# Three quarters of the first adaptive condition on TensorE, one quarter on VectorE

## The chip, the cores and the metric

The kernel runs on one core of a Trainium2 chip. The metric is device time in microseconds (us). Engines are called PE (TensorE, whose weight loads are listed apart as PEld), DVE (VectorE), ACT (ScalarE), POOL (GpSimd) and SP, which issues most DMA transfers.

## The reference

One block of a latent backbone: adaptive normalisation, two kinds of scanned attention, an output projection and a gated feed-forward. 2048 latent tokens of width 1024 and 256 context tokens go through the same weights. Only its beginning matters here:

```python
mod_x = (jax.nn.silu(c) @ w_ada[l] + b_ada[l])[:, None, :]
mod_c = jax.nn.silu(c_ctx) @ w_ada[l] + b_ada[l]
shx1, scx1, gx1, shx2, scx2, gx2 = jnp.split(mod_x, 6, -1)
shc1, scc1, gc1, shc2, scc2, gc2 = jnp.split(mod_c, 6, -1)
fc = mixer_features(modulate(rmsnorm(h_ctx, g_mix[l]), shc1, scc1), ...)
fx = mixer_features(modulate(rmsnorm(x, g_mix[l]), shx1, scx1), ...)
```

The first of the six parts, the shift, is columns 0 to 1023 of the product, the second, the scale, columns 1024 to 2047. These 2048 columns of `w_ada` (8 MB in fp32) are needed before any token can be normalised; the 4096 others come later and are not touched. There are two vectors to multiply with them, one for the latents and one for the context (c = 0 and c = 1 in the code).

## The kernel before

`w_ada`'s first 2048 columns arrive in eight slices of 128 rows (k = 0 to 7, 1 MB each) in the tiles `area0` to `area3`, two slices to a tile. Each slice has four column blocks of 512. Blocks 0 and 1 (the shift) go to PE: the two vectors, padded to 32 columns in `csl`, are the stationary operand, and the sums over k stand as rows in two PSUM tiles `mrow`. An fp32 matmul of this form shows as two records in the trace. Blocks 2 and 3 (the scale) go to DVE: for each vector and block it multiplies the slice with a scalar per partition and adds it to an accumulator `dacc` (arena tiles 12 to 15, shown as arena_93 to arena_96), four passes a slice. The sum over the partitions is still to be done then.

Meanwhile ACT squares the context (`ctxv`, shown as area_101), POOL adds the squares up, and `rstd` and `diag` make a diagonal matrix of the context's inverse norms (tile gm), which `rows_bc` multiplies with ones on PE to broadcast them over the partitions: `bc_ctx`.

After the last slice PE turns the condition into columns, in one PSUM tile `mps`: the accumulators by 16 matmuls with a column of ones, the rows `mrow` (copied to SBUF by ACT, tiles `mrs`) by 8 matmuls with the identity. DVE adds the bias, which gives `modc`, and makes `a1` and `b1` of it; with them and `bc_ctx` the context is modulated (`modulate`), split in a high and a low part for PE, and multiplied with the first weights: the gate weights and the first key unit (tile w). Between lie the sums over the partitions of the first latent block's squares (`x0s`, arena tiles 4 and 5, shown as arena_85 and arena_86): ACT squares, DVE and POOL add, PE sums.

Every engine runs its instructions in order. Program order is that in which the code issues them, but a scheduler that simulates the engines' times lists them anew before the program is built; so a change at the start may move instructions further on. The tiles of the pool gm (5 buffers), of w (4) and of the raw weights wr (3) are used in turn. The trace gives line 193 to nearly all instructions, a helper's line, so rows are told apart by their tiles.

Of the kernel before, what the change touches and what calls it, by code (L numbers as in the profile page):

```python
# [16 lines left out]
ALU = mybir.AluOpType  # L17

P = 128
D = 1024  # L20
KT = 8
T = 2048
TCX = 256
NB = 4
BT = 512
# [57 lines left out]
def pack(i):  # L83
# [69 lines left out]
    ident=(P, P), mneg=(P, 2, P), lmask=(P, len(LEVELS) * 128), tri=(P, 2 * P))  # L153
# [45 lines left out]
def block_kernel(ctx: ExitStack, tc: tile.TileContext, I, out):  # L199
    nc = tc.nc  # L200
    load = Load()
    V, G, S, PE = [Metered(e, load, k) for e, k in ((nc.vector, "V"), (nc.gpsimd, "G"), (nc.scalar, "S"), (nc.tensor, "PE"))]
# [19 lines left out]
    def ctile(shape, name, dt=F32, pool=const):  # L222
        return pool.tile(shape, dt, name=name)
# [10 lines left out]
    def M_(shape=(P, BT)):  # L234
        return gen.tile(list(shape), F32, name="gm", tag="gm", bufs=BUFS["gm"])
# [11 lines left out]
    def flat(i):  # L247
        return arena[i].rearrange("p a b -> p (a b)")[:, :BT]
# [15 lines left out]
    def MM():  # L264
        return pmm.tile([P, BT], F32, name="mm")

    def PS(shape=(P, BT)):
        return pps.tile(list(shape), F32, name="ps")

    def small(n):  # L270
        return sm.tile([P, n], F32, name=f"sm{n}", tag=f"sm{n}")
# [4 lines left out]
    def loaded(name, shape, dt=F32, pool=const):  # L276
        t = ctile(shape, name, dt, pool)
        dma(t, I[name])
        return t
# [7 lines left out]
    def cs(c):  # L287
        return slice(c * P, (c + 1) * P)

    pc = loaded("pc", [P, NPC])  # L290
    ident = loaded("ident", [P, P])
# [26 lines left out]
    ones = ctile([P, P], "ones")  # L318
# [8 lines left out]
    csl = csl_.rearrange("p (k c) -> p k c", c=32)  # L327
# [58 lines left out]
    def rstd(t, n, r):  # L386

        nj = n // P
        ps = PS()
        ts = t if isinstance(t, list) else [t]  # L390
        for j in range(nj):
            for i, t in enumerate(ts):
                PE.matmul(ps[:, 2 * j:2 * j + 2], t[:, cs(j)], ones[:, 0:2], start=(i == 0), stop=(i == len(ts) - 1))
        V.tensor_scalar(r[:, :nj], ps[:, 0:2 * nj:2], 1.0 / D, EPS, ALU.mult, ALU.add)
        G.tensor_tensor(r[:, :nj], r[:, :nj], mhalf[:, :nj], ALU.pow)

    def diag(t, n, r):
        for j in range(n // P):
            V.tensor_scalar(t[:, cs(j)], ident, r[:, j:j + 1], None, ALU.mult)

    def rows_bc(t, n):
        bc = PS()
        PE.matmul(bc[:, :n], ones, t[:, :n], start=True, stop=True)
        return bc
# [12 lines left out]
    def sq_sums(x, n, engs):  # L417

        ts = [flat(4 + k)[:, :n] for k in range(KT)]
        m = len(engs)  # L420
        for k in range(KT):
            S.activation(ts[k], x(k), AF.Square)
            if k >= m:
                engs[k % m].tensor_tensor(ts[k % m], ts[k % m], ts[k], ALU.add)
        return ts[:m]

    mrow = [MM(), MM()]
    dacc = {(q, c): flat(12 + 2 * q + c) for q in range(2) for c in range(2)}
    rc_ = small(4)
    late_x = []  # L430
    for k in range(KT):
        ak = ada[k // 2][:, k % 2]
        for q in range(2):
            m = PE.matmul(mrow[q][0:32], csl[:, k], ak[:, q * BT:(q + 1) * BT], start=(k == 0), stop=(k == KT - 1))
            for c in range(2):
                a = ak[:, D + q * BT:D + (q + 1) * BT]
                if k == 0:
                    V.tensor_scalar(dacc[q, c], a, csl[:, k, c:c + 1], None, ALU.mult)
                else:
                    V.scalar_tensor_tensor(dacc[q, c], a, csl[:, k, c:c + 1], dacc[q, c], ALU.mult, ALU.add)  # L440
        late_x.append(m)
        if k == 3:
            ct_ = sq_sums(lambda i: ctxv[:, i], TCX, [G])
        if k == 6:
            rstd(ct_, TCX, rc_)
            ct_ = M_()
            diag(ct_, TCX, rc_)
    bc_ctx = rows_bc(ct_, TCX)
    modc = ctile([P, 48, 2], "modc")
    mps = PS()  # L450
    for u in range(8):
        for c in range(2):
            o = 16 + 4 * u + 2 * c
            PE.matmul(mps[:, o:o + 2], dacc[u // 4, c][:, cs(u % 4)], ones[:, 0:2], start=True, stop=True)
    mrs = [M_() for _ in range(2)]
    for q in range(2):
        S.copy(mrs[q][0:32], mrow[q][0:32])
    for u in range(8):
        PE.matmul(mps[:, 2 * u:2 * u + 2], mrs[u // 4][0:32, cs(u % 4)], ident[0:32, 0:2], start=True, stop=True)
    bada = pc[:, C_BADA:C_BADA + 16, None].broadcast_to([P, 16, 2])  # L460
    V.tensor_tensor(modc[:, 8:16], mps[:, 16:48].rearrange("p (u c two) -> p u c two", c=2, two=2)[:, :, :, 0],
                    bada[:, 8:16], ALU.add)
    a1 = ctile([P, 2, KT], "a1")
    b1 = ctile([P, 2, KT], "b1")
    for c in (1, 0):
# [1729 lines left out]
```

## Time and profile before

| | |
|---|---|
| median of three runs | 2883.23 us (2871.2 to 2886.63) |
| profiled execution | 2878.33 us, of which 2876.5 us are the profile's span |
| busy over the span | PE 92%, DVE 65%, POOL 60%, ACT 48% |
| chain that ended last | PE 51%, DVE 18%, DMA 13%, ACT 6% |
| mean granted clock of PE | 0.96 of full speed |

The shares are means over stages with different limits. The change lies in the first 50 us, and there the time from the last slice of `w_ada` to the first matmul on the context is to be read, engine by engine; the stage after that shows what an earlier start of it is worth.

### The profile page before, as it was taken

The numbers are of one execution on the slowest core, as the hardware profiler recorded it, in microseconds if no ns is written. First come the engines' busy times: TensorE is split into PE (matmuls) and PEld (weight loads), VectorE is DVE, ScalarE is ACT, GpSimd is POOL, SyncE is SP. The second block draws the span as 40 slices with busy tenths as digits, with TensorE's granted clock in tenths as the row PEclk, the third lists the DMA queues.
The fourth block names the chain that finished last, engine by engine and source line by source line (L and its number), as shares of the span: only waits on it lengthen the run. The fifth ranks groups of instructions, "written<-read, shape, count | busy, mean of one in ns | idle before, by whom it ended". The sixth has DMA issues, their size and how long they took to land.

```text
span 2876.5 us, 44314 instructions
## 1 busy us (share of the span) xinstructions
PE 2634.8 (92%) x13592; PEld 2212.8 (77%) x13592; DVE 1877.0 (65%) x3893; ACT 1388.7 (48%) x3367; POOL 1725.9 (60%) x2323
## 2 busy tenths in 40 slices
PE   6999989898989888988999999889997999998898
PEld 4888979787878767876788888667785888886777
DVE  7578778865864345788788544777656444447775
ACT  4666654544545556665556334334443333343343
POOL 4676533345455345758666556777756655557773
PEclk7999999899999999998999999999998999999999
DMA  6764534476666777753334322423572332224212
GB/s 262 241 192 144 161 81 135 134 209 205 195 201 195 212 211 227 240 154 95 119 117 141 128 86 79 140 73 97 190 251 77 116 101 88 85 76 144 73 59 88
DMA packets 295916, 418.44 MB, mean 145 GB/s; under 512 B 38654, under 2 KB 181278, under 8 KB 292992
## 3 DMA queue, kind: packets, MB, share of 16 engines
q1 hardware_dynamic: 288320, 397.42, 44.6%
q0 software_dynamic: 7360, 18.19, 1.9%
q8 instruction: 108, 1.77, 0.3%
q14 instruction: 128, 1.05, 0.1%
HBM read 304.99 MB, written 110.49 MB: 144 GB/s over the span
## 4 chain that ended last, share of the span: by engine, by line
PE 51%; DVE 18%; DMA 13%; issue 6%; ACT 6%; POOL 4%; SPq 1%; DVEq 0%; POOLq 0%; ACTq 0%
PE mm L193 46%; DVE arena L193 6%; DVE area L193 6%; PE ps L193 5%; DVE gm L193 4%; ACT arena L193 2%; POOL w L193 2%; DVE xall L193 2%; DMA area<-in_wada_dram 2%; DMA arena<-d_nm 2%; DMA arena<-d_bt 1%; POOL arena L193 1%; SPq L207 1%; ACT area L193 1%; ACT ps L193 1%
## 5 line engine op out<-in xcount | busy, mean ns | idle before, releaser
L193 PE MATMUL mm<-area,w 128*128 128x512 f32 (+2 forms) x8264 | 1988.0, 398 | 96.5 <-DVE area L193 39.3
L193 PEld LDWEIGHTS mm<-area,w 128*128 128x128 f32 (+1 forms) x8264 | 1554.1, 193 | 440.2 <-DVE area L193 40.8
L193 POOL TENSOR_TENSOR w<-area,w 128x256 fp32r<-128x256 f32 x572 | 453.2, 815 | 294.7 <-ACT w L193 271.6
L193 POOL TENSOR_TENSOR w<-wr,w 128x256 fp32r<-128x256 f32 (+2 forms) x484 | 386.6, 818 | 163.1 <-ACT w L193 146.9
L193 POOL TENSOR_TENSOR arena<-arena 128x128 f32<-128x128 f32 (+1 forms) x520 | 232.9, 471 | 192.2 <-DMA arena<-d_bt 52.7
L193 ACT CAST w<-area 128x512 fp32r<-128x512 f32 x286 | 177.0, 620 | 287.4 <-PE mm L193 260.8
L193 PE MATMUL ps<-arena,arena 128*128 128x129 f32 (+2 forms) x1700 | 232.4, 294 | 60.3 <-ACT arena L193 20.1
L193 PEld LDWEIGHTS ps<-arena,arena 128*128 128x128 f32 (+1 forms) x1700 | 210.8, 194 | 83.3 <-ACT arena L193 26.6
L193 PE MATMUL mm<-w,area 128*128 128x256 f32 x1728 | 228.5, 289 | 2.8 <-DVE gm L193 1.4
L193 ACT CAST w<-wr 128x512 fp32r<-128x512 f32 (+3 forms) x272 | 158.0, 583 | 146.5 <-PE mm L193 74.4
L193 DVE TENSOR_TENSOR area<-area 128x512 f32<-128x512 f32 (+1 forms) x214 | 160.0, 761 | 104.1 <-DMA area<-in_wgu_dram 58.1
L193 PEld LDWEIGHTS mm<-w,area 128*128 128x128 f32 x1728 | 216.7, 194 | 5.3 <-DVE gm L193 1.6
L193 DVE TENSOR_TENSOR arena<-ps,arena 64x128 f32<-64x128 f32 (+1 forms) x512 | 154.9, 303 | 94.3 <-ACT ps L193 67.5
L193 DVE TENSOR_TENSOR gm<-mm,gm 128x512 f32<-128x512 f32 (+3 forms) x136 | 93.0, 684 | 160.2 <-PE mm L193 131.6
L193 DVE SCALAR_TENSOR_TENSOR gm<-mm,pc,gm 128x441 f32<-128x441 f32 (+4 forms) x328 | 187.7, 596 | 8.0 <-ACT edge L193 5.2
L193 DVE SCALAR_TENSOR_TENSOR area<-mm,modc,area 128x512 f32<-128x512 f32 (+1 forms) x184 | 131.4, 721 | 85.4 <-PE mm L193 85.3
L193 DVE TENSOR_TENSOR arena<-arena,arena 128x256 f32<-128x256 f32 (+3 forms) x170 | 128.6, 766 | 57.7 <-ACT arena L193 27.8
L193 ACT COPY gm<-mm 128x512 f32<-128x512 f32 (+3 forms) x183 | 104.0, 571 | 118.2 <-PE mm L193 115.6
L193 ACT ACTIVATE ps<-arena 128x256 f32<-128x256 f32 x224 | 85.2, 385 | 129.4 <-DVE xall L193 89.4
L193 PEld LDWEIGHTS ps<-arena,xall 128*128 128x128 f32 x896 | 117.9, 197 | 26.7 <-issue 5.0
L193 PE MATMUL ps<-arena,xall 128*128 128x64 f32 x896 | 122.1, 277 | 16.2 <-DVE xall L193 6.9
L193 DVE TENSOR_TENSOR xall<-ps,arena 64x128 f32<-64x128 f32 x448 | 129.2, 289 | 7.0
(179 smaller groups left out, 3046.7 us busy)
## 6 DMA issues: line engine op xcount, KB each, us to landing
area<-in_wgu_dram SPq DMA_DIRECT2D x170, 256.0 KB, 2.7
d_ff<-gm SPq DMA_DIRECT2D x88, 256.0 KB, 2.0
arena<-d_ff SPq DMA_DIRECT2D x88, 256.0 KB, 2.8
wr<-in_win_dram SPq DMA_DIRECT2D x72, 256.0 KB, 4.0
wr<-in_wout_dram SPq DMA_DIRECT2D x64, 256.0 KB, 3.7
arena<-d_kq SPq DMA_DIRECT2D x112, 128.0 KB, 3.0
area<-in_wada_dram SPq DMA_DIRECT2D x24, 512.0 KB, 5.1
arena<-d_bt SPq DMA_DIRECT2D x80, 128.0 KB, 2.8
```

Source lines behind the costliest of these rows:

```text
L193: return f(out, *args, **kw)
L207: return nc.sync.dma_start(o, i)
```

## The change

PE takes three column blocks (the shift, and the first half of the scale), DVE one. The rows of PE are turned into columns first, then the accumulators, and `bc_ctx` is issued after both instead of before. The bias is added in three pieces instead of two.

```diff
--- before.py
+++ after.py
@@ -424,20 +424,20 @@
                 engs[k % m].tensor_tensor(ts[k % m], ts[k % m], ts[k], ALU.add)
         return ts[:m]
 
-    mrow = [MM(), MM()]
-    dacc = {(q, c): flat(12 + 2 * q + c) for q in range(2) for c in range(2)}
+    mrow = [MM() for _ in range(3)]
+    dacc = [flat(12 + c) for c in range(2)]
     rc_ = small(4)
     late_x = []
     for k in range(KT):
         ak = ada[k // 2][:, k % 2]
-        for q in range(2):
+        for q in range(3):
             m = PE.matmul(mrow[q][0:32], csl[:, k], ak[:, q * BT:(q + 1) * BT], start=(k == 0), stop=(k == KT - 1))
-            for c in range(2):
-                a = ak[:, D + q * BT:D + (q + 1) * BT]
-                if k == 0:
-                    V.tensor_scalar(dacc[q, c], a, csl[:, k, c:c + 1], None, ALU.mult)
-                else:
-                    V.scalar_tensor_tensor(dacc[q, c], a, csl[:, k, c:c + 1], dacc[q, c], ALU.mult, ALU.add)
+        for c in range(2):
+            a = ak[:, 3 * BT:]
+            if k == 0:
+                V.tensor_scalar(dacc[c], a, csl[:, k, c:c + 1], None, ALU.mult)
+            else:
+                V.scalar_tensor_tensor(dacc[c], a, csl[:, k, c:c + 1], dacc[c], ALU.mult, ALU.add)
         late_x.append(m)
         if k == 3:
             ct_ = sq_sums(lambda i: ctxv[:, i], TCX, [G])
@@ -445,21 +445,22 @@
             rstd(ct_, TCX, rc_)
             ct_ = M_()
             diag(ct_, TCX, rc_)
-    bc_ctx = rows_bc(ct_, TCX)
     modc = ctile([P, 48, 2], "modc")
     mps = PS()
-    for u in range(8):
+    mrs = [M_() for _ in range(3)]
+    for q in range(3):
+        S.copy(mrs[q][0:32], mrow[q][0:32])
+    for u in range(12):
+        PE.matmul(mps[:, 2 * u:2 * u + 2], mrs[u // 4][0:32, cs(u % 4)], ident[0:32, 0:2], start=True, stop=True)
+    for u in range(12, 16):
         for c in range(2):
-            o = 16 + 4 * u + 2 * c
-            PE.matmul(mps[:, o:o + 2], dacc[u // 4, c][:, cs(u % 4)], ones[:, 0:2], start=True, stop=True)
-    mrs = [M_() for _ in range(2)]
-    for q in range(2):
-        S.copy(mrs[q][0:32], mrow[q][0:32])
-    for u in range(8):
-        PE.matmul(mps[:, 2 * u:2 * u + 2], mrs[u // 4][0:32, cs(u % 4)], ident[0:32, 0:2], start=True, stop=True)
+            o = 24 + 4 * (u - 12) + 2 * c
+            PE.matmul(mps[:, o:o + 2], dacc[c][:, cs(u % 4)], ones[:, 0:2], start=True, stop=True)
+    bc_ctx = rows_bc(ct_, TCX)
     bada = pc[:, C_BADA:C_BADA + 16, None].broadcast_to([P, 16, 2])
-    V.tensor_tensor(modc[:, 8:16], mps[:, 16:48].rearrange("p (u c two) -> p u c two", c=2, two=2)[:, :, :, 0],
-                    bada[:, 8:16], ALU.add)
+    V.tensor_tensor(modc[:, 12:16], mps[:, 24:40].rearrange("p (u c two) -> p u c two", c=2, two=2)[:, :, :, 0],
+                    bada[:, 12:16], ALU.add)
+    V.tensor_tensor(modc[:, 8:12], mps[:, 16:24].rearrange("p (u c) -> p u c", c=2), bada[:, 8:12], ALU.add)
     a1 = ctile([P, 2, KT], "a1")
     b1 = ctile([P, 2, KT], "b1")
     for c in (1, 0):
```

On PE, around the last slices (area_105 holds slices 6 and 7; arena_85 is the context's sum of squares; `ps<-ident,gm` turns rows into columns, `ps<-gm,ones` is bc_ctx, `ps<-ones,arena_93` an accumulator's sum):

```order
 L193 MATMUL ps<-ones,arena_85 128x2 x2
-L193 MATMUL mm<-area_105,arena_81 32x512 x4
+L193 MATMUL mm<-area_105,arena_81 32x512 x6
+L193 MATMUL ps<-ident,gm 128x2 x4
 L193 MATMUL ps<-gm,ones 128x256
+L193 MATMUL ps<-ident,gm 128x2 x8
 L193 MATMUL ps<-ones,arena_93 128x2
 L193 MATMUL ps<-ones,arena_94 128x2
```

Twelve transposing matmuls stand now ahead of the accumulators' sums, around the broadcast; before, eight stood behind the sums, of which there were 16 and are now 8.

On DVE, the last two slices of the accumulation (sm holds the context's inverse norms, the rows with ident make the diagonal matrix):

```order
-L193 TENSOR_SCALAR sm_168<-ps 128x2
+L193 TENSOR_SCALAR sm_169<-ps 128x2
+L193 TENSOR_SCALAR gm<-ident,sm_169 128x128 x2
 L193 SCALAR_TENSOR_TENSOR arena_93<-area_105,arena_81,arena_93 128x512
 L193 SCALAR_TENSOR_TENSOR arena_94<-area_105,arena_81,arena_94 128x512
-L193 SCALAR_TENSOR_TENSOR arena_95<-area_105,arena_81,arena_95 128x512
-L193 SCALAR_TENSOR_TENSOR arena_96<-area_105,arena_81,arena_96 128x512
-L193 TENSOR_SCALAR gm<-ident,sm_168 128x128 x2
 L193 TENSOR_TENSOR arena_85<-arena_85,arena_87 128x512
```

The diagonal matrix is made ahead of the last slice's passes instead of behind them, and two of four passes a slice are gone.

On ACT, where the context's modulation ends (area_101 and its high part), in the program before (area_416 are the tokens of latent block 1, whose squares are summed; `gm<-mm 32x256` copies the gates' first result; area_280 and area_472 are block 0 and its high part; CAST w makes the high part of a weight tile):

```order
L193 ACTIVATE area_101<-area_101,b_274 128x256 x2
L193 ACTIVATE area_416,rx_336<-area_416 128x1024 x2
L193 COPY gm<-mm 32x256
L193 ACTIVATE area_416,rx_336<-area_416 128x1024 x2
L193 CAST arena_329<-gm 98x512
L193 ACTIVATE gm<-mm,pc 16x256
L193 CAST w<-wr 128x512 x2
L193 ACTIVATE area_472<-area_280,b_274 128x512
```

and in the changed one, where area_408 are the same tokens and area_272 and area_464 the same block and its high part:

```order
L193 ACTIVATE area_101<-area_101,b_266 128x256 x2
L193 COPY gm<-mm 32x256
L193 ACTIVATE area_408,rx_328<-area_408 128x1024 x2
L193 ACTIVATE gm<-mm,pc 16x256
L193 ACTIVATE area_464<-area_272,b_266 128x512
L193 ACTIVATE area_408,rx_328<-area_408 128x1024 x2
L193 ACTIVATE area_464<-area_272,b_266 128x512
L193 CAST arena_321<-gm 98x512
L193 ACTIVATE area_464<-area_272,b_266 128x512
L193 CAST w<-wr 128x512
```

All four squaring passes and three activations of block 0 stand now between the copy and the next weight cast; before it was two passes and none.

Beyond the start both programs hold the same instructions on every engine, but for two more table loads on ACT. Their order differs in places: on PE in the first sixth of its instructions and between a fifth and a half of them, by up to some 70 places; from the middle to the end it is the same. On SP transfers move by up to 27 places.

## Rows read from the trace of the kernel before

**Rows 1.** The page: span, and busy time of each engine with its instructions.

```profile
span 2876.5 us, 44314 instructions
...
PE 2634.8 (92%) x13592; PEld 2212.8 (77%) x13592; DVE 1877.0 (65%) x3893; ACT 1388.7 (48%) x3367; POOL 1725.9 (60%) x2323
```

**Rows 2.** TensorE in the timeline: start us, us, engine, what, count, idle before it.

```profile
6.39 7.04 PE L193 MATMUL mm<-area,arena 128*32 128x512 f32 x12 [6.39 <-DMA area<-in_wada_dram]
...
21.18 1.90 PE L193 MATMUL mm<-area,arena 128*32 128x512 f32 x4 [0.54 <-DMA area<-in_wada_dram]
24.05 0.61 PE L193 MATMUL ps<-ones,arena 128*128 128x2 f32 x4 [0.96 <-POOL arena L193]
24.58 3.62 PE L193 MATMUL mm<-area,arena 128*32 128x512 f32 x8
34.38 1.22 PE L193 MATMUL ps<-gm,ones 128*128 128x256 f32 x2 [6.17 <-DVE gm L193]
...
42.15 3.57 PE L193 MATMUL ps<-ident,gm 32*128 32x2 f32 x16
45.65 3.58 PE L193 MATMUL ps<-ones,arena 128*128 128x2 f32 x16
49.09 6.11 PE L193 MATMUL mm<-area,w 128*112 128x256 f32 x28
...
59.38 6.40 PE L193 MATMUL mm<-area,w 128*128 128x256 f32 x36 [3.33 <-ACT w L193]
```

**Rows 3.** One of TensorE's first weight loads in the timeline.

```profile
8.07 0.18 PEld L193 LDWEIGHTS mm<-area,arena 128*32 128x32 f32 x1 [0.68 <-issue]
```

**Rows 4.** VectorE in the timeline, from the last slices to the condition.

```profile
29.17 3.74 DVE L193 SCALAR_TENSOR_TENSOR arena<-area,arena,arena 128x512 f32<-128x512 f32 x4
32.84 1.49 DVE L193 TENSOR_SCALAR gm<-ident,sm 128x128 f32<-128x128 f32 x2
...
45.76 0.26 DVE L193 TENSOR_TENSOR modc<-ps,pc 128x16 f32<-128x16 f32 x2 [9.24 <-PE ps L193]
```

**Rows 5.** ScalarE in the timeline, 26 to 60 us.

```profile
28.24 0.57 ACT L193 COPY gm<-mm 32x512 f32<-32x512 f32 x1 [0.28 <-PE mm L193]
28.72 4.52 ACT L193 ACTIVATE arena<-area 128x512 f32<-128x512 f32 x8
...
51.59 1.04 ACT L193 ACTIVATE area<-area 128x1024 f32<-128x1024 f32 x1
52.53 0.19 ACT L193 ACTIVATION_READ_ACCUMULATOR area<-area 128x1 f32 x1
...
55.23 0.36 ACT L193 COPY gm<-mm 32x256 f32<-32x256 f32 x1 [1.47 <-PE mm L193]
...
58.21 0.47 ACT L193 ACTIVATE gm<-mm,pc 16x256 f32<-16x256 f32 x1
58.70 1.14 ACT L193 CAST w<-wr 128x512 fp32r<-128x512 f32 x2
59.75 0.72 ACT L193 ACTIVATE area<-area,b 128x512 fp32r<-128x512 f32 x1
```

**Rows 6.** GpSimd in the timeline: the last sum of block 0's squares.

```profile
36.23 1.41 POOL L193 TENSOR_TENSOR arena<-arena,arena 128x512 f32<-128x512 f32 x1
```

**Rows 7.** Stretches: length, busy us of PE, PEld, DVE, ACT, POOL; clock; DMA.

```profile
28.30:34.30 6.00, 0.00 (x0) 0.00 (x0) 6.00 (x10) 5.85 (x12) 4.14 (x3) 0.67 1.06 401
34.30:49.00 14.70, 14.62 (x66) 14.41 (x66) 5.25 (x17) 2.60 (x7) 4.91 (x9) 0.50 0.77 303
56.00:80.00 24.00, 17.55 (x91) 15.09 (x90) 23.71 (x35) 19.60 (x36) 19.77 (x22) 0.79 0.21 69
80.00:100.00 20.00, 19.85 (x97) 16.40 (x98) 11.36 (x14) 9.90 (x20) 12.39 (x14) 1.00 0.76 244
450.00:1600.00 1150.00, 1037.62 (x5663) 884.47 (x5663) 797.34 (x2075) 641.06 (x1871) 639.29 (x1006) 0.96 0.58 175
```

**Rows 8.** Waits between 450 and 1600 us: total us, times, longest.

```profile
POOL arena L193 <- DMA arena<-d_nm: 60.1, 30, 5.5
```

## The prediction

> **What bounds the kernel now.** I read the page first: PE is busy 92% of a span of 2876.5 us [rows 1]. A mean like that says nothing of the first 50 us, so next came PE's own timeline there. The reader should see two gaps in it. Up to 28.2 us PE runs the row matmuls as the slices land: the last eight records start at 24.58 and take 3.62 us. Then nothing for 6.17 us, released by DVE, until the context's broadcast at 34.38 [rows 2]. DVE explains it: its passes over the last slice run from 29.17 for 3.74 us, although PE had finished with that slice at 28.2, and the diagonal matrix follows at 32.84 with 1.49 us [rows 4]. So at this place DVE is the engine that ends last. From 34.38 on PE is the bound, with small matmuls: broadcast, 32 records of sums, 16 of transposes, and DVE waits 9.24 us for them before it can add the bias at 45.76 [rows 2, 4]. Behind them PE sums block 0's squares (45.65, 3.58 us) and starts on the context at 49.09 [rows 2].
>
> The stretches say what the stage after that hangs on: from 56 to 80 us DVE is busy 23.71 of 24 us, PE 17.55 and ACT 19.60; from 80 to 100 PE is busy 19.85 of 20 [rows 7]. And PE waits 3.33 us for a weight tile from ACT before 59.38 [rows 2].
>
> **The change, part by part.** Sixteen of DVE's 32 accumulating passes go. At 3.74/4 = 0.94 us [rows 4] these are some 15 us of DVE work, but most of it ran while slices were still landing; on the path it frees only the gap of 6.17 us.
>
> PE gets 8 more row matmuls, 16 records. With six records a slice instead of four it falls behind the loads. The first four records go at the low rate, 0.18 + 0.68 = 0.86 us apart [rows 3], two more at 1.90/4 = 0.475 [rows 2]: slice 0 ends at 6.39 + 3.44 + 0.95 = 10.8. Five slices of 6 x 0.475 = 2.85 us bring slice 5's end to 25.0; its load was there by 21.18 [rows 2], so no load is waited for. The context's sums take 0.61 (POOL had delivered at 24.05), and slices 6 and 7 twelve records of 3.62/8 = 0.45, 5.4 us. PE ends the rows at 31.1 instead of 28.2: 2.9 us later. This is not hidden; it is paid out of the gap.
>
> DVE is then in time: the sum of squares is on PE at 25.6 instead of before slice 6, the diagonal matrix takes 1.49, the last two passes 1.9 [rows 4]. Even with a microsecond or two for GpSimd's power function between, it is done by 31, when PE has 24 transposing records ahead of the accumulators.
>
> The third copy on ACT starts at 31.1 and takes 0.57 [rows 5]; eight records from the first row tile cover it. Block 0's squares (28.72, 4.52 us [rows 5]) stand behind the copies on ACT and start at 31.7, 2.9 us later; POOL's last sum of them, which ended at 36.23 + 1.41 = 37.6 [rows 6], moves with them to 40.5.
>
> Small records: 24 transposes and 16 sums replace 16 and 32. At the price of the row of transposes, 3.57/16 = 0.22 us [rows 2], that is 5.4 + 3.6 us, with 1.2 for the broadcast 10.1 us, from 31.1 to 41.2. The condition is there at 41.3 instead of 45.76, 4.5 us earlier. POOL's sum (40.5) is just in time, and block 0's 16 records of 3.58 us end at 44.8: the context starts 4.4 us earlier than 49.09.
>
> What is that worth? The copy of the gates' result on ACT moves from 55.23 to 50.8. But the order behind it has changed. Before, the next weight cast began 58.70 - 55.23 = 3.5 us after the copy began. Now copy (0.36), four squaring passes with their reads (4 x 1.04 + 4 x 0.19, less some overlap, 4.9), the gates' activation (0.47), three of block 0's activations (0.72 each) and a cast (0.6, half of 1.14) stand ahead of it [rows 5]: 8.5 us. The cast begins at 59.3, 0.6 later than before, and PE, waiting for it before 59.38 [rows 2], resumes 0.6 later, not 4.4 earlier. Against that, ACT has three activations (2.2 us) behind it that before came after the cast, and DVE, the engine that is busy all the time from 56 to 80, can start on block 0 4.4 us earlier. If DVE's work sets the end of this stage, 4.4 us are kept; if the weight casts do, 0.6 us are lost. The two row readings bound it, and nothing in the rows sits nearer to one than the other, save that ACT's 2.2 us of finished work must come back. I take 2 us kept.
>
> The rest of the program holds the same instructions in another order. The trace of before can't show the new order. I take nothing for it, and as its bounds a tenth of PE's idle time in the reordered stretch: 1150 - 1037.6 = 112 us are idle between 450 and 1600 [rows 7], so 11 us either way. Two more table loads on ACT, which is busy 48% of the span [rows 1], cost nothing where it idles.
>
> **The sum.** Gap -6.2, late rows +2.9, small records -1.2 (10.1 instead of 11.4 from 34.38 to 45.76), start of the context -4.4, kept 2. The profiled execution took 2878.3 us, 1.8 us more than its span, and would take 2876. The median of the runs is 2883.2, 4.9 us above the profiled one, so I predict 2881. The runs shown spread over 15 us, 0.5%, which is about what a measurement can tell from no change.
>
> **A rule weighed.** In the rows PE's clock falls in the gap (mean 0.67 of 2.4 GHz from 28.3 to 34.3) and then stays at 0.50, the level of 1.2 GHz, from 34.3 to 49 us, although PE is busy 14.62 of these 14.7 us with small matmuls [rows 7]. The same kind of record took 0.61/4 = 0.15 us at 24.05, at full clock, against 0.22 [rows 2]. The Trainium skill's "TensorE: Matmul & The Clock Gate", section "Why this matters for your kernels", advises to keep TensorE busy without idle gaps to get and keep the full clock. By that advice the removed gap would keep the clock up; the rows show that busy time of this kind does not bring it up, and whether it holds it up no row shows.
>
> **The rivals.**
>
> *Hidden in part (forecast).* 2881, own range 2872 to 2889. Chance 0.42.
>
> *The whole head gain is kept.* DVE decides from 56 to 80, which its 23.71 of 24 us speak for [rows 7]; against it speaks the late weight cast. 2883.2 - 4.4 = 2879. Chance 0.15.
>
> *The clock stays up.* With no gap, the small records run at 0.15 us: 24 and 16 of them and the broadcast take 6.7 us, to 37.8; now POOL's sum at 40.5 decides, and 16 records of 0.15 end at 43.0, 6.1 us earlier than before. Weight cast 1.1 earlier, middle of the two 3.6: 2880. For it speaks that the gap is gone, against it the 14.7 us at half clock in spite of work [rows 7]. Chance 0.15. The skill's advice above is this rival.
>
> *ACT's order makes it slower.* Place: the four squaring passes ahead of the weight cast at 59 us. If the context starts no earlier than before, because PE's rows or the late squares take more than I think, the cast comes 8.5 - 3.5 = 5 us later, and so does the next unit: 2888. It decides once the gain at the head is under 2 us. Chance 0.10.
>
> *A reordered scan is slower or faster.* SP's transfers move by up to 27 places. Between 450 and 1600 us POOL waits 30 times for loads of d_nm, 60.1 us in all, 2.0 us a time [rows 8]. If the new order delays these by half a microsecond each, that is 15 us: 2898; as much the other way gives 2868. Chance 0.06 and 0.12 (the simulated order was made for an earlier start, which the early part then has). That the change does not do what it says is excluded by the new order: rows and passes are there.
>
> **How the numbers follow.** The likeliest is 2881. The cases of under 5 us all lie between 2872 and 2890 with the spread of the runs; the reordering's bounds of 11 us around 2881 widen this to 2866 and 2893, outside which lie most of the last rival's two ends and little else, under 2 in 10. Faster by over 0.5% (under 2868.8) is the fast end of the reordering and a little of the clock: 0.14. Slower by over 0.5% (over 2897.6) is its slow end: 0.06. Within: 0.80.
>
> **What would show it.** In the new profile the row matmuls should end near 31 and the small records follow without a gap; DVE's bias near 41; the first context matmul near 45; ACT's weight cast near 59, with PE waiting about 8 us for it. Small records of 0.15 instead of 0.22 would be the clock's rival. If PE's long stretch before 100 us begins 4 us earlier, the whole gain was kept. A time outside the range would mean that the order between 450 and 1600 us matters more than the change itself, and would stand in PE's idle time there.

## The result: 0.8% slower

The changed kernel took 2900.23 us in the median of six runs (2893.68 to 2903.5), the kernel before, timed with it, 2876.84 us (2871.16 to 2886.63). The ratio is 1.0079, interval [1.0066, 1.0092]. The prediction, 2881 us between 2866 and 2893 with a chance of 0.06 for slower, was wrong.

What makes it odd stands in the first 60 us. They became better than predicted. TensorE in the timeline of the changed kernel (start us, us, engine, what, count, idle before it):

```profile
24.69 0.61 PE L193 MATMUL ps<-ones,arena 128*128 128x2 f32 x4
25.23 5.34 PE L193 MATMUL mm<-area,arena 128*32 128x512 f32 x12
30.50 1.05 PE L193 MATMUL ps<-ident,gm 32*128 32x2 f32 x8
31.48 0.70 PE L193 MATMUL ps<-gm,ones 128*128 128x256 f32 x2
32.10 1.94 PE L193 MATMUL ps<-ident,gm 32*128 32x2 f32 x16
33.98 2.23 PE L193 MATMUL ps<-ones,arena 128*128 128x2 f32 x16
36.91 0.59 PE L193 MATMUL ps<-ones,arena 128*128 128x2 f32 x2 [0.70 <-DVE arena L193]
38.07 3.15 PE L193 MATMUL ps<-ones,arena 128*128 128x2 f32 x14 [0.57 <-POOL arena L193]
41.08 0.75 PE L193 MATMUL mm<-area,w 128*112 128x256 f32 x2
...
55.20 3.76 PE L193 MATMUL mm<-area,w 128*128 128x256 f32 x14 [7.25 <-ACT w L193]
```

The 6.17 us gap of [rows 2] is gone; the row matmuls end at 30.57 and the small ones follow. The context begins at 41.08 where it began at 49.09, 8.0 us earlier. But the stretch at 55.20, which stood at 59.38 [rows 2], waits 7.25 us for ScalarE's weight tile instead of 3.33, so 4.2 us are left of the 8.0. VectorE and ScalarE at these places, in the same view:

```profile
26.50 0.48 DVE L193 TENSOR_SCALAR gm<-ident,sm 128x128 f32<-128x128 f32 x2 [0.84 <-POOL sm L193]
...
36.78 0.31 DVE L193 TENSOR_TENSOR modc<-ps,pc 128x8 f32<-128x8 f32 x3
```

```profile
47.12 0.36 ACT L193 COPY gm<-mm 32x256 f32<-32x256 f32 x1 [3.26 <-PE mm L193]
...
54.55 0.60 ACT L193 CAST w<-wr 128x512 fp32r<-128x512 f32 x1
```

The condition is there at 36.78 (45.76 before [rows 4]), the copy at 47.12 (55.23 [rows 5]), but the cast only at 54.55 (58.70 [rows 5]).

Where, then, are the 23 us lost? I laid the two traces beside each other, TensorE's records counted from the end (beyond the start the programs hold the same matmuls, though not in the same order). The changed kernel is some 8 us ahead at 43 to 53 us, 4 ahead at 59, level at 85 to 108, 7 behind at 330, 9 behind at 350 to 400, 8 to 16 behind up to 1110, 19 at 1212, 22 to 25 from 1300 to the end. There is no single place. The stretches of the changed kernel (length, busy us of PE, PEld, DVE, ACT, POOL; clock; DMA):

```profile
60.00:300.00 240.00, 214.71 (x1520) 196.72 (x1519) 162.01 (x399) 149.97 (x359) 159.36 (x237) 0.94 0.56 180
450.00:1600.00 1150.00, 1030.45 (x5634) 874.86 (x5633) 789.25 (x2066) 631.66 (x1844) 627.60 (x998) 0.96 0.57 172
```

and the first of them in the kernel before:

```profile
60.00:300.00 240.00, 221.85 (x1581) 202.55 (x1581) 172.44 (x429) 156.62 (x378) 169.35 (x253) 0.95 0.58 185
```

From 60 to 300 us TensorE is busy 7.1 us less than before, and gets through 61 records fewer; from 450 to 1600 us 7.2 us less (1037.62 [rows 7]). Over the whole span its busy time is even longer, 2645.7 against 2634.8 us [rows 1]. Of these 10.9 us the changed head with its 8 more records makes 1.4; from the first context matmul on the same 13491 records took longer, 2612.6 instead of 2603.2 us:

```profile
span 2899.9 us, 44344 instructions
...
PE 2645.7 (91%) x13600; PEld 2212.8 (76%) x13600; DVE 1869.7 (64%) x3878; ACT 1394.3 (48%) x3370; POOL 1723.8 (59%) x2323
```

So idle time grew by 12.5 us and busy time by 10.9. The longer busy time is not a chance of two traces: from the first context matmul on TensorE is busy 2601.0 to 2606.5 us in three traces with the old order throughout (before, `bias_three_pieces`, `new_head_old_order`) and 2612.6 to 2618.4 us in four with the new one (the changed kernel, `split31_old_sequence`, `split22_new_sequence`, `old_head_new_order`); the runs follow below.

### The profile page after: what moved, and what is told of

It is laid out like the page before. It is cut to its first block, busy times and chain, and to the rows that moved or that the text cites. A ratio compares the mean times of both kernels' runs of the same rounds, so it can differ in the third digit from the quotient of the medians.

```text
span 2899.9 us, 44344 instructions
## 1 busy us (share of the span) xinstructions
PE 2645.7 (91%) x13600; PEld 2212.8 (76%) x13600; DVE 1869.7 (64%) x3878; ACT 1394.3 (48%) x3370; POOL 1723.8 (59%) x2323
## 4 chain that ended last, share of the span: by engine, by line
PE 37%; DVE 7%; POOL 2%; DMA 2%; issue 2%; ACT 1%; DVEq 0%; POOLq 0%; ACTq 0%; SPq 0%
PE mm L193 36%; DVE area L193 4%; DVE arena L193 1%; PE ps L193 1%; POOL w L193 1%; DVE gm L193 1%; DMA area<-in_wgu_dram 0%; POOL arena L193 0%; POOL area L193 0%; DMA gm<-d_o 0%; ACT w L193 0%; DVE xall L193 0%; DMA gm<-d_x 0%; ACT area L193 0%; ACT arena L193 0%
## 5 line engine op out<-in xcount | busy, mean ns | idle before, releaser
L193 PE MATMUL mm<-area,w 128*128 128x512 f32 (+1 forms) x8264 | 1992.0, 398 | 99.7 <-DVE area L193 38.5
L193 DVE TENSOR_TENSOR area<-area 128x512 f32<-128x512 f32 (+1 forms) x214 | 164.4, 781 | 111.2 <-DMA area<-in_wgu_dram 57.2
```

The costliest lines, as they stand in the source:

```text
L193: return f(out, *args, **kw)
```

## The experiments

**Theory A:** the head gains, and the order in which the scheduler lists the instructions behind it loses more. **Theory B:** the loss comes from the head itself, from what it computes and when, and from the moved broadcast above all. The twelve kernels besides the changed one were timed in five rounds beside the kernel before, in three series (its medians there 2870.8, 2870.22 and 2872.41 us); the changed kernel's row is the result above. Kernels of different series are compared by their ratios. "Old" and "new" are the orders of the program before and of the changed one; the stretches part at about 300 and 720 us.

| run | head | order to 300 us / to 720 us / behind | median us | ratio to before |
|---|---|---|---|---|
| new_head_old_order | changed | old / old / old (forced) | 2866.61 | 0.9984 [0.9972, 0.9995] |
| new_head_new_old_old | changed | new / old / old (forced) | 2878.74 | 1.0024 [1.0015, 1.0033] |
| new_head_new_new_old | changed | new / new / old (forced) | 2878.92 | 1.0027 [1.0014, 1.0040] |
| new_head_old_old_new | changed | old / old / new (forced) | 2881.55 | 1.0031 [1.0021, 1.0041] |
| new_head_old_new_new | changed | old / new / new (forced) | 2882.25 | 1.0042 [1.0026, 1.0058] |
| changed kernel | changed | new / new / new | 2900.23 | 1.0079 [1.0066, 1.0092] |
| old_head_new_order | before's | new / new / new (forced) | 2898.95 | 1.0100 [1.0082, 1.0118] |
| split31_old_sequence | split only | new / new / new | 2895.97 | 1.0079 [1.0065, 1.0093] |
| split22_new_sequence | sequence only | new / new / new | 2893.21 | 1.0066 [1.0053, 1.0079] |
| bias_three_pieces | before's | old, some places apart | 2871.52 | 1.0001 [0.9989, 1.0013] |
| adders_swapped | changed, one edit | nearly new / old / old | 2880.29 | 1.0031 [1.0017, 1.0045] |
| b1_on_gpsimd | changed, one edit | a third / old / old | 2874.46 | 1.0005 [0.9995, 1.0015] |
| new_order_two_places_undone | changed | new, two places old (forced) | 2891.39 | 1.0069 [1.0049, 1.0089] |

### Head and order exchanged

To force an order, the kernel holds a table of the other program's sequence on each of the five engines, from block 0's load on, and ties each instruction behind its predecessor on its engine. The ties set the order only; no engine waits for another because of them. No run forces a program's own order, so a cost of the ties alone is not measured. Against one that matters speak two pairs below: `adders_swapped`, which forces nothing, has 1.0031 where the forced kernel of nearly the same order has 1.0027, and the forced `new_order_two_places_undone` is no slower than the changed kernel.

```diff
+def pin_order(nc, tc, base):
...
+    left = np.frombuffer(zlib.decompress(base64.b85decode(PIN)), "<i2").astype(np.int64).tolist()
...
+        for a, b in zip(v, v[1:]):
+            tc.add_manual_dep(made[f"I-{base + b}"], f"I-{base + a}", nosync, reason="order of another program")
...
     while any(queue[k] or active[k] for k in KINDS):
         after_step()
+    pin_order(nc, tc, pin_base)
```

The changed head with the old order:

> The changed kernel, with all instructions from block 0's load on forced, engine by engine, into the order that the kernel before has (issue order alone, no added waits). Theory A (the loss of 23 us is the scheduler's new order, the change itself gains at the head): not slower than before, 2865 to 2877 us, the first context matmul at about 41 us. Theory B (the change itself costs the time, through what its earlier start collides with): about 2900 us as the changed kernel.

Measured 0.9984 [0.9972, 0.9995], 2866.61 us. TensorE from 40 us on in this run:

```profile
40.83 0.75 PE L193 MATMUL mm<-area,w 128*112 128x256 f32 x2
41.87 4.74 PE L193 MATMUL mm<-area,w 128*112 128x256 f32 x26 [0.29 <-DVE area L193]
46.44 1.02 PE L193 MATMUL ps<-gm,ones 128*128 128x512 f32 x2
50.79 6.40 PE L193 MATMUL mm<-area,w 128*128 128x256 f32 x36 [3.33 <-ACT w L193]
```

The wait for the weight tile is 3.33 us again, as in [rows 2], and the stretch starts 8.6 us earlier than at 59.38 there. What is left of that at the end is 0.16%, 4 to 5 us in the medians.

The head before with the new order:

> The kernel before, with its old start, and from block 0's load on forced into the order that the changed kernel has. Theory A: about 2900 us or some us more, since the order's loss is there without the head's gain of 8 us. Theory B: 2877 us, as before.

Measured 1.0100 [1.0082, 1.0118], 2898.95 us. The new order loses 1.0% behind the old head, and 0.95% behind the new one (0.9984 to 1.0079). That is theory A, and against B: the order costs 27 to 29 us (of 2870). The change to the head gains 0.16% with the old order, with an interval from 0.05 to 0.28%; the 0.21% between the two heads with the new order is about as large as its own uncertainty.

A part of the order's loss goes with TensorE's clock. Over all runs the mean granted clock was 0.9584 to 0.9593 in the five kernels with the new order throughout (one of them with two places put back), and 0.9611 to 0.9627 in the kernel before and the eight others. With the two levels 1.00 (2.4 GHz) and 0.50 (1.2 GHz) this is 235 to 241 us at the lower level against 214 to 223. My estimate from these numbers is that some 19 us more at half clock, in which half as much gets done, cost up to 9 us of the loss. What in the order lowers the clock no run shows.

### Which stretch of the order

The same table, with the other program's sequence up to or from a place in each engine's list (TensorE's 2000th and 3715th instruction behind block 0's load, near 300 and 720 us). First the old order up to 300 us, then the old order from 720 us on:

> The changed kernel, with the order of the kernel before up to about 300 us and its own order from there on (between 300 and 530 us both orders agree). Theory A: what was lost up to 350 us (from 8 us ahead to 8 us behind in the traces, 16 us) comes back, the loss after 1100 us (12 us) stays: 2884 to 2890 us. Theory B: 2900 us.

> The changed kernel in its own order up to about 720 us and in the order of the kernel before from there to 1400 us, where they come to agree again. Theory A: the loss of 12 us after 1100 us comes back, the early one stays: 2886 to 2890 us. Theory B: 2900 us.

Measured 1.0042 (2882.25 us) and 1.0027 (2878.92 us). Both medians lie below the ranges in us, which I had reckoned from 2877 us for the kernel before; it took 2870.8 in this series. As ratios to 2877 the ranges are 1.0024 to 1.0045 and 1.0031 to 1.0045, so the first holds and the second was missed by 0.04%: the late order costs a little more than I expected. By these runs the early order is worth 0.37%, the late one 0.52%. Whether these add up, and the mirror images:

> The changed kernel with the order behind the start forced: as in the program before up to about 720 us, as in the changed one from there on (there TensorE's projections, mm, stand some 25 matmuls later and the scan's, ps, some 49 earlier than before, for most of the stretch from 770 to 1210 us). Theory A (losses of the stretches add): the whole old order gave 0.9984, the old order from 720 us on gave back 0.0052, so this gives 0.9984 + 0.0052 = 1.0036 (1.002 to 1.005), with the lag behind the old order's trace growing between 750 and 1350 us. Theory C (the middle only loses what the early part set late): 0.998 to 1.000.

> The mirror image: the changed kernel with the changed order up to about 300 us and the old one behind it. Theory A: the old order gave 0.9984, the early part's order costs 0.0037, so 1.002 (1.0005 to 1.0035); the lag behind the old order's trace stands at 10 to 16 us from 320 us to the end. If the early lag is a slack that is made up later (theory D): 0.998 to 1.000.

Measured 1.0031 [1.0021, 1.0041] and 1.0024 [1.0015, 1.0033], against 1.0036 and 1.002 expected. Alone, the late order costs 1.0031 - 0.9984 = 0.47% and the early one 0.40%; the order between 300 and 720 us costs 0.03% (1.0027 to 1.0024) or 0.11% (1.0042 to 1.0031). So the losses add, within the intervals of some 0.1% a run, and neither is slack of the other: theories C (the late part loses only what the early part set late) and D (the early lag is made up later) fall.

What the late stretch's order does to the waits, from 740 to 1340 us (total us, times, longest), first with the old order throughout:

```profile
POOL arena L193 <- DMA arena<-d_nm: 54.5, 27, 5.1
...
ACT ps L193 <- DMA arena<-d_nm: 26.3, 11, 9.8
DVE arena L193 <- ACT ps L193: 23.9, 27, 4.2
```

then with the new order behind 720 us (new_head_old_old_new):

```profile
POOL arena L193 <- DMA arena<-d_nm: 75.3, 31, 7.9
...
DVE arena L193 <- ACT ps L193: 46.9, 27, 6.6
...
ACT ps L193 <- DMA arena<-d_nm: 39.5, 11, 9.1
PEld ps L193 <- issue: 32.2, 16, 4.6
```

By the order itself, for most of 770 to 1210 us TensorE's projection matmuls (mm) stand 25 places later in the new list and the scan's (ps) 49 places earlier on average, and ScalarE's weight casts 30 later. The scan then has fewer projections ahead of it, and its engines wait more for one another. Over all fourteen traces the clearest sign of the late stretch's order is VectorE's wait for ScalarE in the scan (DVE arena <- ACT ps, 740 to 1340 us): 19.6 to 24.9 us in the seven traces with the old order there, 43.7 to 50.8 in the seven with the new one. TensorE's weight loads for the scan (PEld ps <- issue) part likewise, 15.5 to 20.2 against 25.2 to 32.2. GpSimd's wait for the loads of d_nm does not: 46.5 to 67.3 against 57.2 to 79.2. That the scan's place is the mechanism within the stretch fits the rows, but no run moves the two streams alone.

### Two places of the early stretch

The trace of the changed kernel shows two waits there that are longer than before's: for the weight cast (7.25 us against 3.33, above), and at the late condition's sum, for a product that GpSimd makes (5.54 us against 0.50):

```profile
154.23 0.56 PE L193 MATMUL ps<-ones,area 128*128 128x2 f32 x2 [5.54 <-POOL area L193]
```

The new order was forced, with these two places as before (ScalarE and TensorE):

```diff
+ACTIVATE area_408,rx_328<-area_408 128x1024 x2
 COPY gm<-mm 32x256
-ACTIVATE area_408,rx_328<-area_408 128x1024 x2
+CAST w<-wr 128x512
 ACTIVATE gm<-mm,pc 16x256
...
-CAST w<-wr 128x512
```

```diff
+MATMUL mm<-area_289,w 128x256
 MATMUL ps<-ones,area 128x2
...
-MATMUL mm<-area_289,w 128x256 x24
+MATMUL mm<-area_289,w 128x256 x23
```

> The changed kernel in its own order, fixed, save two places at which its trace showed TensorE waiting: on ScalarE the weight cast stands directly behind the copy of the gates' result again, with two of the four squaring passes ahead of the copy (place 1), and on TensorE the late condition's sum and the three sums behind it stand behind the first matmul of the next unit again (place 2). Theory A1 (these two places make the early part's loss of some 11 us): the cast begins near 48.5 instead of 54.55 us, TensorE waits some 2 us instead of 7.25 for it and 0.5 instead of 5.5 for the sum near 154, and 8 to 11 us come back: ratio to before 1.004 to 1.005. Theory A2 (the loss is spread over the order, what comes back at one place is lost at the next): under 4 us come back, ratio 1.0065 to 1.009.

Measured 1.0069 [1.0049, 1.0089]. ScalarE and TensorE in this run:

```profile
48.22 0.61 ACT L193 CAST w<-wr 128x512 fp32r<-128x512 f32 x1
```

```profile
55.31 1.65 PE L193 MATMUL mm<-area,w 128*128 128x256 f32 x6 [4.64 <-ACT w L193]
58.29 4.00 PE L193 MATMUL mm<-area,w 128*128 128x256 f32 x17 [1.32 <-POOL w L193]
...
151.05 0.28 PE L193 MATMUL ps<-ones,area 128*128 128x2 f32 x2
...
170.34 0.56 PE L193 MATMUL ps<-ones,area 128*128 128x2 f32 x2 [4.54 <-POOL arena L193]
```

The cast came at 48.22, 6.3 us earlier, but TensorE had work for eight matmuls and then waited 4.64 us for the next cast; the sum at 151.05 waited no longer, but the one at 170.34 waited 4.54 us. What came back at one place was lost at the next. The median speaks for A2 (under 4 us), but the interval holds 1.0079 too, so that anything came back is not shown; A1's 8 to 11 us (1.004 to 1.005) lie at and beyond its other edge. The early loss hangs on no one wait that I found, and its cause within the order stays open.

### Parts of the change, with the scheduler left free

The split alone, with the sequence of the code as before:

```diff
+    bc_ctx = rows_bc(ct_, TCX)
     modc = ctile([P, 48, 2], "modc")
     mps = PS()
+    for u in range(12, 16):
...
     mrs = [M_() for _ in range(3)]
...
-    for u in range(12, 16):
...
-    bc_ctx = rows_bc(ct_, TCX)
```

> The change's split alone (three column blocks on TensorE, one on VectorE, bias in three pieces), with the code's sequence as before: the context's broadcast first, then the accumulators' sums, then the rows turned into columns. The scheduler lists this program beyond the start in the same order as the changed kernel. Theory A (the order behind the start decides): slower than before like the changed kernel, ratio 1.006 to 1.010, whatever the head gains. Theory B (the head's own sequence decides, the late broadcast above all): without the moved broadcast the loss goes away, ratio 0.997 to 1.000. In the trace A expects the first context matmul near 41 to 43 us as in the changed kernel, and TensorE's wait of some 7 us for the weight cast before about 56 us again.

Measured 1.0079 [1.0065, 1.0093], the number of the changed kernel, with the context at 40.95 us and the wait for the weight tile of 7.25 us again:

```profile
27.92 0.70 PE L193 MATMUL ps<-gm,ones 128*128 128x256 f32 x2
28.55 2.76 PE L193 MATMUL mm<-area,arena 128*32 128x512 f32 x6
...
40.95 0.75 PE L193 MATMUL mm<-area,w 128*112 128x256 f32 x2
...
55.20 3.75 PE L193 MATMUL mm<-area,w 128*128 128x256 f32 x14 [7.25 <-ACT w L193]
```

Theory B's late broadcast is out: it stands here, at 27.92, ahead of the last slice's matmuls, and nothing changes.

The sequence alone, with two blocks for each engine as before:

```diff
-    bc_ctx = rows_bc(ct_, TCX)
     modc = ctile([P, 48, 2], "modc")
     mps = PS()
-    for u in range(8):
...
     mrs = [M_() for _ in range(2)]
...
+    for u in range(8):
...
+    bc_ctx = rows_bc(ct_, TCX)
```

> The change's sequence alone: two blocks on TensorE and two on VectorE as before, but rows turned into columns first, then the accumulators' sums, the broadcast last. The head hardly moves, since VectorE still ends late: the first context matmul between 47 and 50 us. The scheduler's order behind it is a third one, neither that of before nor that of the changed kernel. Theory A: the time is that of a third draw, anywhere within 1% of before, and not to be told from the head; a ratio outside 0.998 to 1.002 with a head that stays would be for it. Theory B (the head's start decides): ratio 0.999 to 1.001.

Measured 1.0066 [1.0053, 1.0079], and this expectation was wrong twice. Behind the start its list is not a third one: on four engines it is the changed kernel's, place for place, and on ScalarE but for one swapped pair. And the head moved:

```profile
28.40 1.94 PE L193 MATMUL ps<-ident,gm 32*128 32x2 f32 x16
30.27 0.38 PE L193 MATMUL ps<-ones,arena 128*128 128x2 f32 x2
30.89 6.56 PE L193 MATMUL ps<-ones,arena 128*128 128x2 f32 x30 [0.23 <-DVE arena L193]
37.32 1.20 PE L193 MATMUL ps<-gm,ones 128*128 128x256 f32 x2
38.31 3.41 PE L193 MATMUL ps<-ones,arena 128*128 128x2 f32 x16
41.58 6.50 PE L193 MATMUL mm<-area,w 128*112 128x256 f32 x28
```

The context starts at 41.58, almost as early as with the whole change. VectorE is as late as before, but TensorE no longer stands waiting for it with the broadcast; it fills the time with the rows and then the accumulators. So either half of the change removes the gap, and either half brings the scheduler to the same new order.

An edit worth nothing at the head, as a control:

```diff
-    V.tensor_tensor(modc[:, 8:16], mps[:, 16:48].rearrange("p (u c two) -> p u c two", c=2, two=2)[:, :, :, 0],
-                    bada[:, 8:16], ALU.add)
+    scale = mps[:, 16:48].rearrange("p (u c two) -> p u c two", c=2, two=2)[:, :, :, 0]
+    V.tensor_tensor(modc[:, 12:16], scale[:, 4:8], bada[:, 12:16], ALU.add)
+    V.tensor_tensor(modc[:, 8:12], scale[:, 0:4], bada[:, 8:12], ALU.add)
```

> The kernel before with one edit that gives and takes next to nothing: the bias of the scale's 8 columns is added in two VectorE instructions of 4 columns in place of one of 8 (one instruction of about 0.13 us more). The scheduler's order behind it is again another one. Theory A: the time is that of another draw, and may differ from before by up to 1% either way although the head is the same to 0.3 us; theory B (a time comes from what is computed at the head): ratio 0.9995 to 1.0005.

Measured 1.0001 [0.9989, 1.0013]. Here too I had expected another order; it is the old one, but for a few places in the middle of TensorE's list. The control shows something else: its profiled execution spans 2867.1 us, 9.4 less than that of before [rows 1], with medians the same. Single traces cannot tell differences of this size, so what I say of differences of under 10 us late in a trace rests on the medians.

Two one-line edits to the changed kernel:

```diff
-    x0s = sq_sums(lambda i: x0[:, i], BT, [V, G])
+    x0s = sq_sums(lambda i: x0[:, i], BT, [G, V])
```

> No forced order: the changed kernel with one edit, the two engines that add up block 0's squares in swapped turns (GpSimd the even, VectorE the odd ones). The scheduler then lists the early part as for the changed kernel, but everything behind it as for the kernel before. Theory A: as the forced order of the same kind, 1.0027 (1.001 to 1.0045); theory B (the head decides): as the changed kernel, 1.008.

```diff
-        V.tensor_copy(b1[:, c], modc[:, 0:8, c])
+        G.tensor_copy(b1[:, c], modc[:, 0:8, c])
```

> No forced order: the changed kernel with b1's two small copies on GpSimd in place of VectorE. The scheduler then lists an early part that is neither of the two orders, and everything behind it as for the kernel before. Theory A: the middle costs nothing, the early part is a third draw between the two known ones: 0.997 to 1.004; theory B (the head decides): as the changed kernel, 1.008.

Measured 1.0031 [1.0017, 1.0045] and 1.0005 [0.9995, 1.0015]. Neither forces anything. Both fall within A's expectations and far from B's 1.008: with the late order back to the old one, half or more of the loss goes, although the second starts the context at 41.07, as early as the changed kernel, and then waits 1.44 us for GpSimd. The best version of all is the changed head with the old order, 0.9984: faster than before by 4 to 5 us (1 to 8 by its interval) and than the changed kernel by 27 (of 2870).

## Why the prediction was wrong

**The step that failed** is "The rest of the program holds the same instructions in another order. ... I take nothing for it, and as its bounds a tenth of PE's idle time in the reordered stretch: ... 11 us either way." The new order costs 0.95 to 1.0%, 27 to 29 us. Three things were wrong in it. The bound was taken from one stretch, 450 to 1600 us; the order up to 300 us, outside it, costs 0.37 to 0.40%, some 11 us, by itself. The stretch behind 720 us alone costs 0.47 to 0.52%, 13 to 15 us, more than the bound. And idle time was the wrong measure: of the 23 us that the profiled span grew, 12.5 are idle and 10.9 are busy time of TensorE; between 450 and 1600 us, where the prediction wanted to see the loss, its idle time grew by 7.2 us. The tenth was a guess about a list that no trace had run. With an order known to differ at 3001 of TensorE's 12100 places, nothing in the rows spoke for zero; the orders run here with the changed head lie between 0.9984 and 1.0079, so, in hindsight, a range of some 1% either way would have held them.

**The rows** end at 30.57 (predicted 31.1), and the diagonal matrix is made at 26.98, in time. Right.

**Small records** were mis-sized: 24 transposes, the broadcast and the first 16 sums take from 30.50 to 36.21, 5.7 us, where I put 10.1 at 0.22 each. They ran at 0.12 to 0.14 us. The clock's rival came true in this, up to 36.2 us; the last 14 sums took 0.22 us each.

**POOL's last sum**, predicted to end at 40.5, began at 36.75 and took 1.26, to 38.0: the squares began 2.4 us later than before (31.09, 28.72 [rows 5]), but their last sum ended only 0.4 us later. I had moved the sum by the whole shift of the squares, but before it had also stood behind a wait of 1.80 us for VectorE, whose adds came after the late diagonal matrix [rows 4]. First before, then the changed kernel, where this wait is gone:

```profile
35.84 0.31 POOL L193 MEMSET arena<- 2x256 f32 x1 [1.80 <-DVE arena L193]
```

```profile
36.75 1.26 POOL L193 TENSOR_TENSOR arena<-arena,arena 128x512 f32<-128x512 f32 x1
```

**The context's start:** 41.08 against 44.8, so -8.0 and not -4.4; the last two points make up the difference.

**The weight cast** stands 7.4 us behind the copy (8.5 predicted, 3.5 before), and TensorE waits 7.25 us (8 predicted). The mechanism was right; with the larger gain ahead of it TensorE resumes 4.2 us earlier instead of 0.6 later. That is more than the 2 us that I took. With the old order TensorE resumes 8.6 us earlier here, and 0.16%, 4 to 5 us, is left in the medians.

**Of the rivals** the one of a slower reordered scan, 2898 us with a chance of 0.06, came nearest. Its sign and its cause (the order) were right, its place only in part, and its time by luck. GpSimd's waits for d_nm between 450 and 1600 us did rise from 60.1 us [rows 8] to 75.1, by the 15 us that I had used:

```profile
POOL arena L193 <- DMA arena<-d_nm: 75.1, 28, 7.9
```

But the control `bias_three_pieces`, with the old order and before's time, has 72.2 us of them, and `split22_new_sequence`, at 1.0066, has 59.8: these waits don't tell the two orders apart. And the order up to 300 us costs nearly as much as the one behind 720 us, and there is no wait for d_nm in it. The rival of ScalarE's order, 2888, did not come about: it wanted a context no earlier than before, and the context was 8.0 us earlier. The late cast that it names is there, but the cast still came 4.2 us earlier than before, and putting it back gave little or nothing.

**The rule weighed.** I had set the Trainium skill's advice to keep TensorE busy ("TensorE: Matmul & The Clock Gate", "Why this matters for your kernels") against a row of 0.50 in spite of busy small matmuls. The rows here agree with it in part. Without the gap the granted clock of the changed kernel stayed at 1.00 from 28.3 to 34.3 us, where it had been 0.67 [rows 7]. But its mean from 30.5 to 36.2 us is 0.94, with TensorE busy 5.70 of 5.70 us: it fell between 34.3 and 36.2, before the first gap, and stood at 0.50 behind it:

```profile
28.30:34.30 6.00, 6.00 (x35) 3.84 (x33) 1.17 (x3) 4.85 (x10) 0.95 (x1) 1.00 1.06 403
30.50:36.20 5.70, 5.70 (x43) 5.26 (x42) 2.96 (x3) 5.60 (x12) 2.77 (x2) 0.94 1.08 409
36.20:41.10 4.90, 3.62 (x18) 3.53 (x17) 4.90 (x15) 2.74 (x8) 4.45 (x9) 0.50 1.01 423
```

## What to carry to other kernels

Where a scheduler lists the program anew, a change has two effects: what it does in its place, and which list it brings about. Here the first was worth -0.16% and the second +1.0%. Compare the lists before you trust a local gain, and time the change with the old list forced as well as with the new one; without that, the head's gain (8 us at the context, 4 to 5 at the end) and the order's loss of 27 could not have been told apart here. And when the list differs in a quarter of its places, do not put its cost at zero; the lists run here with the changed head spread over nearly 1%. A look at the waits did not find the early loss: undoing the two plainest of them gave back 0.1% (3 us) by the ratios, less than the interval.

## What the runs showed of the hardware that I had not expected

TensorE's clock fell without a gap in the changed kernel (rows above), and a second run shows a fall with hardly any. In `split22_new_sequence` the row matmuls end at 28.4 us and small ones follow, with 0.23 us idle at most. Three stretches of that run (columns as above):

```profile
24.80:28.40 3.60, 3.60 (x10) 0.83 (x9) 3.60 (x7) 0.57 (x1) 0.00 (x0) 1.00 1.00 423
28.40:30.80 2.40, 2.26 (x19) 2.15 (x18) 2.40 (x6) 2.29 (x5) 1.16 (x1) 1.00 0.98 395
30.80:37.30 6.50, 6.41 (x30) 6.41 (x31) 5.78 (x8) 3.49 (x7) 4.09 (x4) 0.50 1.07 418
```

The granted clock goes from 1.00 (2.4 GHz) to 0.50 (1.2 GHz) while TensorE is busy 2.26 of 2.40 us and then 6.41 of 6.50 us, with the transposes and the 128x2 sums. The same sums took 2.23/16 = 0.14 us in the changed kernel at 33.98 and 6.56/30 = 0.22 us here. In both runs TensorE was busy with such records when the clock fell; in the changed kernel the last 14 of them, at 38.07, took 0.22 us each as well.
